# Hybrid decoder block on one core: high parts first in the products of sums, and the opening stage written in another order

## The chip, the cores and the metric

The kernel runs on one core of one Trainium2 chip. The metric is the time of one launch in device microseconds. Before the change it was 1389.92 us, the median of three runs (1389.33 to 1391.17).

## The reference

One decoder layer for 1024 positions of width 1024, in float32. Cut to what matters here:

```python
h = rms_norm(x, mix_norm_g)
z_a, q, k, v, gate_logits = jnp.split(h @ w_in, splits, axis=-1)
y_a = chunked_spatial_gating(gelu(z_a), gmlp_norm_g, w_spatial, b_spatial)
q, k = apply_partial_rope(q, cos, sin), apply_partial_rope(k, cos, sin)
y_b = dilated_mixture_attention(q, k, v)
merged = sigmoid(g_a) * (y_a @ w_branch_a) + sigmoid(g_b) * (y_b @ w_branch_b)
x = x + merged @ w_out
a, val = jnp.split(rms_norm(x, ffn_norm_g) @ w_up, 2, axis=-1)
x = x + (gelu(causal_dwconv3(a)) * val) @ w_down
return rms_norm(x, final_norm_g)
```

## The kernel before

**Numbers in two parts.** A float32 operand is split into a high part (a copy in the matmul's type, written by ScalarE) and a low part (operand minus high, written by VectorE, in later stages by GpSimd too). A product of a 512-deep slice is 12 matmuls into one PSUM bank: for each of 4 slices of 128 rows the passes high·high, high weight·low input, low weight·high input. The helper `to_parts` (from line 164) writes both parts of a weight.

**Fewer products.** The large projections use seven products of half-size blocks instead of eight. They are called P1, P6, P2, P7, P5, P4, P3. Their left operands are blocks of the input (A11, A12, A22) or sums of blocks (S1 to S4), their right operands blocks or differences of the weight. P2 accumulates into the bank of P1, P4 into that of P7 and P3 into that of P5. Between two such products VectorE or ScalarE has to fold the first one's result out of the bank: after P7 with `add(c22, c12, src)` (line 537), after P5 with `add(c22, c22, src)` (line 539), after P1 with a copy (line 530). So P4 waits for the fold of P7, and P3 for that of P5.

**The input projection** has pairs of 128 output columns. Pairs 0 and 1 are computed plainly, as four half products of 24 matmuls each (`plain_step`, line 562 on), because they need nothing but the raw input times the norm's gain; the row norms are applied later. From pair 2 on (`FIRST = 2`) `in_product` (line 498) computes the seven products. Its inputs are sums of the normalised input, so the norms have to be known: `square_row` and `root` (ScalarE and GpSimd), `diagonal` (four small diagonal matrices), `spread` (TensorE multiplies them by ones, so that each row's factor lies along the free side, tile `rs_bc`), `scale_x` (VectorE), `x_sum` and `x_sum_dma` (sums of blocks, two of them by a DMA that accumulates), `parts_of` (high and low parts of each block).

**What else stands in the opening.** `rot_tables` (line 2176) makes the sine and cosine tables of the rotary embedding: a chain of small VectorE steps, given out by `some(n)`; two sines on ScalarE; 16 small copies on ScalarE that widen the tables (`wide`, line 2238); and four turns, each four transposes on TensorE and a copy on ScalarE (`turns`, line 2255). `turn_v` (line 618) transposes the results of pairs 0, 1 and 2 by blocks into two shared PSUM tiles (`tr`), which ScalarE empties, with GELU for pairs 0 and 1 (line 628), by a copy for pair 2 (line 633). Then `norm_v` (squares on ScalarE, two GpSimd steps, a scaling on VectorE) and `spatial` (small matmuls into the same two PSUM tiles, emptied by VectorE, line 669).

**What sets the order.** Each engine runs its instructions in one order. On TensorE the order is that of the program throughout (`pe_order`). On VectorE and ScalarE it is the written one while `ordered` is open, that is through `beginning()` and the first seven products of pair 2 (`ORDERED = 6`). After that a scheduler orders these two engines, until a written order is opened again later (the opening of the up projection has one). `after(lag, fn)` queues work that is written `lag` ticks later; `tick()` comes every six matmuls of a product. `meanwhile(i)` is called after product i of the seven-product order. SyncE issues the loads in the order written. The up projection (`up_product`, line 1776) has the same seven products, its opening (`beginning_up`, from line 1889) in a written order: `up_ahead(loads, ops)` runs loads and weight parts ahead, `low(n)` writes n low parts that are waiting.

Of the kernel before, what the change touches and what calls it, by code (L numbers as in the profile page):

```python
# [20 lines left out]
P = 128  # L21
# [72 lines left out]
def block_kernel(  # L94
# [61 lines left out]
        return ap.bitcast(F32)  # L156

    PASSES = ((0, 0), (0, 1), (1, 0))


    waiting = []
# [45 lines left out]
    def after(lag, fn):  # L207
        pending.setdefault(clock[0] + lag, []).append(fn)
# [53 lines left out]
    def in_load(n, which):  # L262
        st = wt.tile([P, KT, P], F32, name=f"wr_{n}_{which}", tag="wr")
        nc.sync.dma_start(st, w_in[2 * n + which])
        raws[n, which] = st
# [63 lines left out]
    def load_x(h, kts):  # L329
        for kt in kts:  # L330
            nc.sync.dma_start(x_half(kt, h), xt[kt, :, h * HALF : (h + 1) * HALF])
# [4 lines left out]
    def load_rows(h):  # L336
        for b in range(4):
            nc.sync.dma_start(rows_of[b], x_t[:, 4 * h + b, :])
# [6 lines left out]
        load_x(0, range(k * QK, (k + 1) * QK))  # L345
    in_load(0, 1)
    load_x(1, range(KT))
    in_load(1, 0)
    load_rows(0)
    in_load(1, 1)  # L350

    nc.vector.memset(mhalf, -0.5)
# [41 lines left out]
    def quarter(i, j, kt):  # L394
        return X[:, j * QK + kt, (lower, upper)[i]]
# [36 lines left out]
    def parts_of(name, kts=range(QK)):  # L432
        i, j = {"A11": (0, 0), "A12": (0, 1), "A22": (1, 1), "S1": (1, 1), "S2": (0, 0),
                "S3": (1, 0), "S4": (0, 1)}[name]
        srcs = [Z[:, kt] if name == "S1" else quarter(i, j, kt) for kt in range(QK)]
        staggered((lambda: None, *in_left(name, kt, srcs[kt])) for kt in kts)
# [17 lines left out]
    def scale_x(h, kt, bc):  # L454
        xs = x_half(kt, h)
        nc.vector.scalar_tensor_tensor(xs, xs, chan[:, kt : kt + 1], bc, ALU.mult, ALU.mult)
# [41 lines left out]
    def in_product(n, name):  # L498
        opened = name not in SHARED
        if not opened:  # L500
            acc = in_banks[n, SHARED[name]]
        elif name == "P1" or n >= 3:
            acc = acc_tile(f"in_{n}_{name}")
        else:
            acc = ps_d.tile([P, HALF], F32, name=f"in_{n}_{name}", tag="dn")
        in_banks[n, name] = acc
        op = in_ops.pop((n, name))
        for kt in range(QK):
            for i, (w, a) in enumerate(PASSES):
                nc.tensor.matmul(  # L510
                    acc, op[:, w, kt, :], left[LEFT[name], kt][:, a, :],
                    start=opened and kt == 0 and i == 0,
                    stop=kt == QK - 1 and i == 2,
                    skip_group_check=not opened,
                )
            if kt % 2 == 1:
                tick()
        kind, _ = PAIRS[n]
        func = FUNC.get(kind, AF.Copy)
        src = in_turn(n, acc)  # L520
        c11, c12, c21, c22 = (c_half(n, i, h) for h in range(2) for i in range(2))
        add = nc.vector.tensor_tensor

        def final(i, h, t):
            if func != AF.Copy:
                nc.scalar.activation(t, t, func)
            in_final(n, i, h)

        if name == "P1":
            nc.scalar.activation(c12, src, AF.Copy)  # L530
        elif name == "P6":
            add(c12, c12, src, ALU.add)
        elif name == "P2":
            nc.scalar.activation(c11, src, func)
            in_final(n, 0, 0)
        elif name == "P7":
            add(c22, c12, src, ALU.add)  # L537
        elif name == "P5":
            add(c22, c22, src, ALU.add)
            final(1, 1, c22)  # L540
        elif name == "P4":
            add(c21, c12, src, ALU.add)
            final(0, 1, c21)
        else:
            add(c12, c12, src, ALU.add)
            final(1, 0, c12)
# [31 lines left out]
    def plain_final(n, h, i):  # L578
        nc.scalar.activation(c_half(n, i, h), plain_banks[n, h, i], AF.Copy)
# [468 lines left out]
    def beginning():  # L1048

        chain, wide, turns = rot_tables(  # L1050
            nc, lent, [[YC[:, i, lower], YC[:, i, upper]] for i in range(2)],
            tr_tile, ident, positions, YC,
        )
        chain = iter(chain)

        def some(n):
            for _, fn in zip(range(n), chain):
                fn()

        def weight(n, k, i):  # L1060
            hi, lo = plain_op(n, k, i)
            hi()
            lo()

        raw = {(h, kt): raw_left(h, kt) for h in range(2) for kt in range(KT)}

        def raw_parts(h, kt):
            for fn in raw[h, kt]:
                fn()

        def product(n, h, i, ks=(0, 1)):
            for k in ks:
                for kt in range(QK):
                    plain_step(n, h, i, k, kt)

        warm_up(12)
        some(5)
        for k in range(2):
            weight(0, k, 0)
            for kt in range(k * QK, (k + 1) * QK):  # L1080
                raw_parts(0, kt)
            product(0, 0, 0, (k,))
        some(2)
        weight(0, 0, 1)
        weight(0, 1, 1)
        plain_final(0, 0, 0)
        product(0, 0, 1)
        for kt in range(KT):
            raw_parts(1, kt)
        product(0, 1, 0)  # L1090
        plain_final(0, 0, 1)
        weight(1, 0, 0)
        weight(1, 1, 0)
        for b in range(4):
            square_row(0, b)
        load_rows(1)
        root(0)
        some(14)
        diagonal(0)
        plain_final(0, 1, 0)  # L1100
        weight(1, 0, 1)
        weight(1, 1, 1)
        product(0, 1, 1, (0,))
        for kt in range(QK):
            plain_step(0, 1, 1, 1, kt)
            if kt == 2:
                bc0 = spread(0)
        for kt in range(KT):
            scale_x(0, kt, bc0)
        plain_final(0, 1, 1)  # L1110
        for b in range(4):
            square_row(1, b)
        root(1)
        parts_of("A11")
        product(1, 0, 0)
        diagonal(1)
        bc1 = spread(1)
        for kt in range(QK):
            scale_x(1, kt, bc1)
            scale_x(1, kt + QK, bc1)  # L1120
            x_sum(1, kt)
            if kt % 2 == 1:
                x_sum_dma(3, kt // 2)
        plain_final(1, 0, 0)
        product(1, 0, 1)
        plain_final(1, 0, 1)
        parts_of("A12")
        in_ahead(0, 9, 2)
        product(1, 1, 0)
        plain_final(1, 1, 0)  # L1130
        for kt in range(2):
            x_sum(2, kt)
        parts_of("S2", range(2))
        product(1, 1, 1)
        in_ahead(0, 9, 3)
        for kt in range(2, QK):
            x_sum(2, kt)
        parts_of("S2", range(2, QK))
        plain_final(1, 1, 1)
        for k in range(2):  # L1140
            x_sum_dma(4, k)
        return some, wide, turns

    def meanwhile(i):
        if i == 0:
            parts_of("S3")
        elif i == 1:
            parts_of("S1")
        elif i == 2:
            parts_of("A22")  # L1150
        elif i == 3:
            parts_of("S4")
            x_stack.close()
            zv["pool"] = zv_stack.enter_context(
                tc.tile_pool(name="zvp", bufs=1, reuse_waits="tile")
            )
            open_zv()
            for b in range(0, NB, 2):
                after(1 + b // 2, lambda b=b: turn_v(1, C[1], b))
                after(5 + b // 2, lambda b=b: turn_v(0, C[0], b))  # L1160
        elif i == ORDERED:
            some(99)
            for fn in wide:
                fn()
        elif i == ORDERED + 2:
            for fn in turns:
                fn()

    ordered = ExitStack()
    ordered.enter_context(  # L1170
# [3 lines left out]
    for i, (n, name) in enumerate(in_order):  # L1174
        in_ahead(i, 9, 4 if i else 2)
        if PAIRS[n][0] == "zu" and name == "P1":
            for c in range(2 * PAIRS[n][1], 2 * PAIRS[n][1] + 2):
                nc.sync.dma_start(ya[:, c, :], mixd[c])
        in_product(n, name)
        meanwhile(i)  # L1180
        if i == ORDERED:
            ordered.close()
# [593 lines left out]
    def up_product(ff, name, beside=None):  # L1776
# [6 lines left out]
            acc = banks[ff, SHARED[name]]  # L1783
        banks[ff, name] = acc
        op = ops.pop((ff, name))
        for kt in range(QK):
            for i, (w, a) in enumerate(PASSES):
                nc.tensor.matmul(  # L1788
                    acc, op[:, w, kt, :], left[LEFT[name], kt][:, a, :],
                    start=opened and kt == 0 and i == 0,  # L1790
                    stop=kt == QK - 1 and i == 2,
                    skip_group_check=not opened,
                )
            if kt % 2 == 1:
                tick()
        u2, v, c21, c12 = u2s[ff % 2], vs_[ff % 2], c21s[ff % 2], c12s[ff % 2]
        ge0, ge1 = ge_of(ff, 0), ge_of(ff, 1)
# [91 lines left out]
    def beginning_up():  # L1889
# [79 lines left out]
        up_product(2, "P7")  # L1969
        up_ahead(18, 16)  # L1970
        up_product(2, "P5")
        up_ahead(18, 17)
        low(1)
        first_taps(2)
        up_product(2, "P4", lambda: up_ahead(20, 19))
        low(1)
# [334 lines left out]
```

## Time and profile before

| | |
|---|---|
| three runs | 1389.33, 1391.17, 1389.92 us |
| the profiled execution | 1391.06 us |
| its span, first to last instruction | 1389.1 us |
| mean granted TensorE clock | 0.996 |
| instructions | 19247 |
| HBM | 167.77 MB read, 64.29 MB written |

Views give times in us from the span's start. A row of the timeline gives start, duration, engine, line, operation, output and inputs, shape and count; in brackets the time that the engine had been idle and what ended that. Durations of one instruction overlap the next one's by a little, since the ends of pipelined instructions are modelled: twelve matmuls that start 0.227 us apart are shown as 2.88 us. A row of the windows gives for each engine the busy time and the number of instructions in that stretch, then the granted clock and the DMA engines' share. PEq, SPq and the like are sequencers; PEld is TensorE loading weights.

### The profile page before, as it was taken

How to read it: one execution, taken by the hardware profiler on the slowest of the kernel's cores; microseconds unless marked ns; L12 is line 12 of the kernel's file. 1: busy time of each engine (PE TensorE's matmuls, PEld its weight loads, DVE VectorE, ACT ScalarE, POOL GpSimd, SP SyncE). 2: the span in 40 equal slices, each digit the busy share in tenths (PEclk: the TensorE clock that was granted, in tenths of full speed). 3: DMA queues.
4: the chain of work that ended last, by engine and by line, in shares of the span. 5: the costliest groups of instructions: out<-in, count | busy, mean ns of one | idle time of the engine just before them, and what ended most of it. 6: DMA issues, size and time to landing. Idle time of an engine off the chain costs nothing.

```text
span 1389.1 us, 19247 instructions
## 1 busy us (share of the span) xinstructions
PE 1364.6 (98%) x6434; PEld 1130.7 (81%) x6434; DVE 1030.6 (74%) x1880; ACT 655.1 (47%) x1289; POOL 298.1 (21%) x295
## 2 busy tenths in 40 slices
PE   9889999999999999999999999999999999999997
PEld 7767888888888888888788878888888888888886
DVE  7868677686877987867889887766766667676674
ACT  7583355555544333634646444333433335455443
POOL 0111000000221000120001146655566553000003
PEclk9999999999999999999999999999999999999999
DMA  9424535354435997694843133333323327986563
GB/s 352 89 65 130 167 109 169 115 167 134 130 116 193 329 307 256 216 300 140 287 133 104 39 117 103 106 107 113 107 103 110 122 84 254 385 322 221 196 206 122
DMA packets 143875, 237.01 MB, mean 171 GB/s; under 512 B 13728, under 2 KB 57504, under 8 KB 143776
## 3 DMA queue, kind: packets, MB, share of 16 engines
q1 hardware_dynamic: 141248, 231.53, 49.5%
q0 software_dynamic: 1088, 2.10, 0.9%
q10 hardware_dynamic: 1440, 2.16, 0.4%
q8 instruction: 51, 0.84, 0.2%
q14 instruction: 48, 0.39, 0.1%
HBM read 167.77 MB, written 64.29 MB: 167 GB/s over the span
## 4 chain that ended last, share of the span: by engine, by line
PE 85%; DVE 6%; ACT 3%; issue 2%; POOL 2%; DMA 2%; SPq 0%; POOLq 0%; ACTq 0%; DVEq 0%
PE in_P L510 25%; PE uP L1788 19%; PE dn L2046 13%; PE up L1788 8%; PE pa L1260 5%; PE wo_P L1621 4%; PE pl L571 2%; PE pu L1767 2%; PE pb L1260 1%; PE pu L851 1%; DMA ld<-scr 1%; PE pp L835 1%; DVE G L166 1%; PE pm L660 1%; POOL st L903 1%
## 5 line engine op out<-in xcount | busy, mean ns | idle before, releaser
L510 PE MATMUL in_P<-R,G 128*128 128x512 f32 x1008 | 243.8, 394 | 1.8 <-ACT C L530 1.8
L510 PEld LDWEIGHTS in_P<-R,G 128*128 128x128 f32 x1008 | 185.4, 188 | 38.5 <-ACT C L530 2.2
L2046 PE MATMUL dn<-R 128*128 128x512 f32 x924 | 209.6, 389 | 0.0
L2046 PEld LDWEIGHTS dn<-R 128*128 128x128 f32 x924 | 173.4, 188 | 36.0
L165 ACT ACTIVATE G<-wr 128x512 fp32r<-128x512 f32 x126 | 79.1, 630 | 150.4 <-PE in_P L510 114.4
L165 ACT ACTIVATE R<-up 128x512 fp32r<-128x512 f32 x130 | 78.8, 627 | 125.1 <-DVE up L278 40.9
L510 PE MATMUL in_P<-G,G 128*128 128x512 f32 x504 | 124.1, 397 | 2.3 <-DVE C L537 2.3
L1788 PE MATMUL up<-G,R 128*128 128x512 f32 x504 | 121.4, 391 | 1.7 <-DVE R L166 1.7
L1788 PE MATMUL uP<-G,R 128*128 128x512 f32 x504 | 121.2, 389 | 0.0
L1788 PE MATMUL uP<-R 128*128 128x512 f32 x504 | 121.1, 389 | 0.0
L1788 PEld LDWEIGHTS up<-G,R 128*128 128x128 f32 x504 | 94.5, 188 | 22.7 <-DVE R L166 2.2
L510 PEld LDWEIGHTS in_P<-G,G 128*128 128x128 f32 x504 | 93.7, 190 | 21.1 <-ACT G L405 2.5
L1788 PEld LDWEIGHTS uP<-G,R 128*128 128x128 f32 x504 | 94.5, 188 | 19.8 <-issue 0.2
L1788 PEld LDWEIGHTS uP<-R 128*128 128x128 f32 x504 | 94.6, 188 | 19.6
L166 DVE TENSOR_TENSOR G<-wr,G 128x512 fp32r<-128x512 f32 x126 | 87.9, 699 | 24.2 <-ACT G L165 24.0
L166 POOL TENSOR_TENSOR R<-up,R 128x512 fp32r<-128x512 f32 x55 | 84.0, 1527 | 74.5 <-ACT R L165 74.5
L166 DVE TENSOR_TENSOR R<-up,R 128x512 fp32r<-128x512 f32 x75 | 63.0, 841 | 16.1 <-ACT R L165 15.9
L165 ACT ACTIVATE R<-db 128x512 fp32r<-128x512 f32 x77 | 48.1, 626 | 56.3 <-PE dn L2046 45.3
L166 DVE TENSOR_TENSOR R<-db,R 128x512 fp32r<-128x512 f32 x77 | 53.7, 701 | 25.8 <-ACT R L165 25.7
L1260 PE MATMUL pa<-R,G 128*128 128x512 f32 x288 | 67.9, 389 | 0.0
L1260 PEld LDWEIGHTS pa<-R,G 128*128 128x128 f32 x288 | 54.1, 188 | 11.2
L510 PE MATMUL in_P<-G 128*128 128x512 f32 x252 | 62.2, 393 | 0.0
(279 smaller groups left out, 2396.5 us busy)
## 6 DMA issues: line engine op xcount, KB each, us to landing
wr<-in_w_in_dram SPq DMA_DIRECT2D x45, 512.0 KB, 4.1
up<-in_w_up_dram SPq DMA_DIRECT2D x44, 512.0 KB, 3.5
dA<-gd SPq DMA_DIRECT2D x55, 256.0 KB, 5.1
wd<-in_w_down_dram SPq DMA_DIRECT2D x44, 256.0 KB, 5.5
wT<-wd SPq DMA_DIRECT2D x44, 256.0 KB, 3.7
dS<-gS SPq DMA_DIRECT2D x44, 256.0 KB, 4.2
db<-wT SPq DMA_DIRECT2D x44, 256.0 KB, 4.2
gd<-Y SPq DMA_DIRECT2D x42, 256.0 KB, 2.0
```

The lines of the kernel that those rows point to most:

```text
L165: nc.scalar.activation(hi, src, AF.Copy)
L166: fn = lambda: lo_eng.tensor_tensor(lo, src, f32(hi), ALU.subtract)
L510: nc.tensor.matmul(acc, op[:, w, kt, :], left[LEFT[name], kt][:, a, :], start=opened and kt == 0 and i == 0, stop=kt == QK - 1 and i == 2, ...
L571: nc.tensor.matmul(acc, plain_ops[n, k, i][:, w, kt, :], raw_x[h, k * QK + kt][:, a, :], start=k == 0 and kt == 0 and p == 0, stop=k == 1 ...
L660: nc.tensor.matmul(pm[:, o : o + P], v[:, c * P : (c + 1) * P], wspT[:, c * 2 // 3, :], start=True, stop=True,)
L835: nc.tensor.transpose(pp[:, i * P : (i + 1) * P], self.pr[:, h, s * P : (s + 1) * P], ident)
L851: nc.tensor.matmul(pu[:, h * HD : (h + 1) * HD], self.pT[:, i, :], vt[:, h * HD : (h + 1) * HD], start=i % n == 0, stop=i % n == n - 1,)
L1260: nc.tensor.matmul(acc, unit[a][kt // 4][:, kt % 4, :], two(R, 8 * h + kt)[:, b, :], start=n == 0 and i == 0, stop=n == len(kts) - 1 and i ...
L1621: nc.tensor.matmul(acc, left[LEFT[name], kt][:, a, blk * P : (blk + 1) * P], out_ops[s][:, w, :], start=name not in SHARED and kt == 0 and ...
L1767: nc.tensor.matmul(acc, plain_up[which, k][:, w, kt, :], left[f"A{h + 1}{k + 1}", kt][:, a, :], start=n == 0 and i == 0, stop=n == KT - 1 ...
L1788: nc.tensor.matmul(acc, op[:, w, kt, :], left[LEFT[name], kt][:, a, :], start=opened and kt == 0 and i == 0, stop=kt == QK - 1 and i == 2, ...
L2046: nc.tensor.matmul(accs[blk], dops[s][:, 0, a, blk * P : (blk + 1) * P], dops[s][:, 1, w, :], start=SEQ[j] not in CONTINUES and kt == 0 an ...
```

## The change

Within each product of `in_product` and `up_product` the twelve matmuls come in another order: four high·high, then four low weight·high input, then four high weight·low input. In the opening, two loads change places and several steps move: the weights of pair 1, the first spread, the squares of the second half, the parts of A11, the second diagonal, the second spread, and P1 of pair 2, which now stands between the two halves of the last plain product. The transposes of pairs 1 and 0 are written four ticks later, the parts of S1 and A22 and the four table turns at other products. In the up projection one weight is loaded and split earlier.

```diff
+    HIGH_FIRST = [(w, a, kt) for w, a in ((0, 0), (1, 0), (0, 1)) for kt in range(D // P // 2)]
...
     load_x(1, range(KT))
+    load_rows(0)
     in_load(1, 0)
-    load_rows(0)
     in_load(1, 1)
...
-        for kt in range(QK):
-            for i, (w, a) in enumerate(PASSES):
-                nc.tensor.matmul(
-                    acc, op[:, w, kt, :], left[LEFT[name], kt][:, a, :],
...
-            if kt % 2 == 1:
+        for i, (w, a, kt) in enumerate(HIGH_FIRST):
+            nc.tensor.matmul(
+                acc, op[:, w, kt, :], left[LEFT[name], kt][:, a, :],
...
+            if i % 6 == 5:
                 tick()
...
         plain_final(0, 0, 1)
-        weight(1, 0, 0)
-        weight(1, 1, 0)
         for b in range(4):
             square_row(0, b)
         load_rows(1)
         root(0)
-        some(14)
+        some(5)
+        weight(1, 0, 0)
+        weight(1, 1, 0)
+        some(11)
         diagonal(0)
         plain_final(0, 1, 0)
...
             plain_step(0, 1, 1, 1, kt)
-            if kt == 2:
+            if kt == 0:
                 bc0 = spread(0)
         for kt in range(KT):
             scale_x(0, kt, bc0)
+        for b in range(2):
+            square_row(1, b)
         plain_final(0, 1, 1)
-        for b in range(4):
+        for b in range(2, 4):
             square_row(1, b)
         root(1)
-        parts_of("A11")
+        a11 = [in_left("A11", kt, quarter(0, 0, kt)) for kt in range(QK)]
+        for hi, lo in a11[:2]:
+            hi()
+            lo()
+        diagonal(1)
+        for hi, lo in a11[2:]:
+            hi()
+            lo()
         product(1, 0, 0)
-        diagonal(1)
+        plain_step(1, 0, 1, 0, 0)
         bc1 = spread(1)
...
-        product(1, 0, 1)
+        for n in range(1, KT):
+            plain_step(1, 0, 1, n // QK, n % QK)
...
-        product(1, 1, 1)
+        product(1, 1, 1, (0,))
         in_ahead(0, 9, 3)
+        in_product(FIRST, "P1")
+        product(1, 1, 1, (1,))
...
     def meanwhile(i):
         if i == 0:
             parts_of("S3")
-        elif i == 1:
+            in_ahead(1, 9, 4)
             parts_of("S1")
-        elif i == 2:
+        elif i == 3:
             parts_of("A22")
-        elif i == 3:
             parts_of("S4")
...
-                after(1 + b // 2, lambda b=b: turn_v(1, C[1], b))
-                after(5 + b // 2, lambda b=b: turn_v(0, C[0], b))
+                after(5 + b // 2, lambda b=b: turn_v(1, C[1], b))
+                after(9 + b // 2, lambda b=b: turn_v(0, C[0], b))
         elif i == ORDERED:
             some(99)
             for fn in wide:
                 fn()
-        elif i == ORDERED + 2:
-            for fn in turns:
-                fn()
+        elif ORDERED + 2 < i < ORDERED + 7:
+            turns.pop(0)()
...
-        in_product(n, name)
+        if i:
+            in_product(n, name)
...
         up_product(2, "P5")
-        up_ahead(18, 17)
-        low(1)
+        up_ahead(20, 18)
+        low(2)
         first_taps(2)
```

The loop of `up_product` changes as that of `in_product` does.

More of the change, by code (lines that the diff above doesn't have):

```diff
@@ L507, in in_product @@
         op = in_ops.pop((n, name))
-        for kt in range(QK):
-            for i, (w, a) in enumerate(PASSES):
-                nc.tensor.matmul(
-                    acc, op[:, w, kt, :], left[LEFT[name], kt][:, a, :],
[L512 to L515, printed above, removed]
-            if kt % 2 == 1:
+        for i, (w, a, kt) in enumerate(HIGH_FIRST):
+            nc.tensor.matmul(
+                acc, op[:, w, kt, :], left[LEFT[name], kt][:, a, :],
+                start=opened and i == 0,
+                stop=i == len(HIGH_FIRST) - 1,
+                skip_group_check=not opened,
+            )
+            if i % 6 == 5:
                 tick()
@@ L1785, in up_product @@
         op = ops.pop((ff, name))
[L1786 to L1794, printed above, removed]
+        for i, (w, a, kt) in enumerate(HIGH_FIRST):
+            nc.tensor.matmul(
+                acc, op[:, w, kt, :], left[LEFT[name], kt][:, a, :],
+                start=opened and i == 0,
+                stop=i == len(HIGH_FIRST) - 1,
+                skip_group_check=not opened,
+            )
+            if i % 6 == 5:
                 tick()
```

## The prediction, made before the changed kernel ran

> **What bounds the kernel.** I read the page first, then the waits of TensorE, then windows of the first 140 us, then the timeline of each engine there, and from the built program of the changed kernel the order of each engine and what each instruction waits for. Page, waits and windows:
>
> ```profile
> PE 1364.6 (98%) x6434; PEld 1130.7 (81%) x6434; DVE 1030.6 (74%) x1880; ACT 655.1 (47%) x1289; POOL 298.1 (21%) x295
> PE 85%; DVE 6%; ACT 3%; issue 2%; POOL 2%; DMA 2%; SPq 0%; POOLq 0%; ACTq 0%; DVEq 0%
> PE in_P L510 <- DVE C L537: 2.3, 1, 2.3
> PE in_P L510 <- ACT C L530: 1.8, 1, 1.8
> PE rs_bc L391 <- ACT C L385: 1.8, 1, 1.8
> PE up L1788 <- DVE R L166: 1.7, 1, 1.7
> PE rot L2255 <- ACT YC L2256: 1.4, 1, 1.4
> PE vt L623 <- ACT V L628: 1.3, 1, 1.3
> PE rot L2255 <- ACT YC L2238: 1.1, 1, 1.1
> 76.00:83.00 7.00, 5.72 (x19) 4.26 (x18) 5.96 (x10) 3.49 (x9) 0.00 (x0) 0.52 0.26 87
> 90.00:100.00 10.00, 7.31 (x45) 5.67 (x44) 4.58 (x16) 9.66 (x30) 0.00 (x0) 1.00 0.00 1
> 120.00:130.00 10.00, 10.00 (x60) 7.75 (x59) 9.47 (x22) 1.75 (x3) 0.00 (x0) 1.00 0.44 124
> ```
>
> TensorE is busy for 98% of the span, and from about 100 us on it hardly stops. So whatever the opening gains or loses reaches the end unchanged, unless a later wait swallows it. Six of the waits lie between 38 and 99 us and make 1.8 + 1.8 + 2.3 + 1.3 + 1.1 + 1.4 = 9.7 us. The clock was 0.52 for the 7 us behind two of them: busy 5.72 us at half speed, about 2.5 us lost. I put 1 us more for the modelled ends, since each wait is counted from an end that lies 0.16 us (2.88 - 12 x 0.227) behind the time when the next matmul could have started. That is about 13 us which the change can win there, and 1.7 us at the up projection.
>
> **The change part by part. Order inside a product.** It touches 2 x 1764 = 3528 matmuls.
>
> ```profile
> L510 PE MATMUL in_P<-R,G 128*128 128x512 f32 x1008 | 243.8, 394 | 1.8 <-ACT C L530 1.8
> L2046 PE MATMUL dn<-R 128*128 128x512 f32 x924 | 209.6, 389 | 0.0
> L1621 PE MATMUL wo_P<-R,G 128*128 128x512 f32 x72 | 19.9, 400 | 0.4 <-ACT Y L1589 0.4
> 19.33 2.88 PE L571 MATMUL pl<-G 128*128 128x512 f32 x12
> 22.05 2.88 PE L571 MATMUL pl<-R,G 128*128 128x512 f32 x12
> ```
>
> Two of three neighbours in the old order share their weight, in the new one none does. The down projection (line 2046) has neighbours that never share it, at 389 ns: so I take 0. The ends are 5 ns less for the input products (1764 x 5 ns = 9 us gained) and the 400 ns of line 1621 (3528 x 6 ns = 21 us lost). What the order does is to need the low weight at the fifth matmul instead of the third and the low inputs at the ninth to twelfth. The high inputs are all needed by the fourth (0.7 us in) instead of the tenth. A product takes 22.05 - 19.33 = 2.72 us.
>
> **Rows ahead of pair 1's weights.**
>
> ```profile
> 24.64 1.06 ACT L366 ACTIVATE YC<-YC 128x1024 f32<-128x1024 f32 x1 [1.39 <-DMA YC<-in_x_dram]
> 18.00:28.00 10.00, 10.00 (x46) 8.29 (x45) 7.20 (x20) 8.48 (x17) 0.92 (x2) 1.00 1.03 396
> 27.28 1.03 POOL L374 TENSOR_TENSOR rs_x<-me_x,mhalf 128x4 f32<-128x4 f32 x1
> 20.68 1.29 DVE L559 TENSOR_TENSOR G<-wr,G 128x512 fp32r<-128x512 f32 x2
> 23.79 0.62 DVE L2193 TENSOR_TENSOR ones<-ones 128x128 f32<-128x128 f32 x2
> 28.35 0.88 DVE L383 TENSOR_SCALAR C<-ident,rs_x 128x128 f32<-128x128 f32 x4 [2.63 <-POOL rs_x L374]
> 27.49 2.20 PE L571 MATMUL pl<-R,G 128*128 128x512 f32 x9
> 29.53 1.05 PE L391 MATMUL rs_bc<-C,ones 128*128 128x128 f32 x8
> ```
>
> The queue is full there (396 GB/s, 1.3 us per 512 KB tile). In the trace the third row tile lands at 24.6, with pair 1's weight ahead of it. In the changed kernel the fourth lands at 24.6, the last square ends at 25.8 instead of 26.8, and the weight lands at 25.7. But VectorE now has the weight's low parts ahead of 11 table steps, and those ahead of the first diagonal. It waits for the weight's high part (25.8 + 0.6), does two low parts (1.29) and 11 steps (some 0.28 each, 3.1 with the gaps): 30.8 instead of 28.35. TensorE reaches the spread after three matmuls of the half that starts at 27.49, at 28.2, and waits until about 31.0. **+2.8 us**, where the trace has no wait. Cover for this there is none: all of the changed TensorE order stands behind.
>
> **Second spread, and P1 between the halves.** The squares of the second half are no longer queued behind the eviction alone, and the second spread comes three matmuls later. By my count its diagonals end at 39.5 and TensorE arrives at 40.2, so the 1.8 us there go. P1 ends 2.7 us before the plain product does, time enough for its eviction (0.6 us, line 530), so the next 1.8 us go too. The last plain half ends at 59.5.
>
> **VectorE's chain to the folds.** The stretch from the second scaling to the fold of P5 has the same instructions as before, in nearly the same order:
>
> ```profile
> 39.90 1.41 DVE L456 SCALAR_TENSOR_TENSOR X<-X,chan,rs_bc 128x512 f32<-128x512 f32 x2 [0.78 <-PE rs_bc L391]
> 57.73 1.29 DVE L465 TENSOR_TENSOR X<-X,YC 128x512 f32<-128x512 f32 x2
> 66.23 2.50 DVE L412 TENSOR_TENSOR G<-YC,G 128x512 fp32r<-128x512 f32 x4 [1.32 <-ACT G L411]
> 77.92 0.68 DVE L539 TENSOR_TENSOR C<-C,in_P 128x512 f32<-128x512 f32 x1
> 75.14 1.96 PE L510 MATMUL in_P<-G,G 128*128 128x512 f32 x6 [2.33 <-DVE C L537]
> ```
>
> It begins at 41.4 instead of 39.90 (the spread ends at 41.2), and is 1.5 us late until 59.25. Then a table load on ScalarE no longer stands ahead of S1's high parts, and the 1.3 us wait goes. From there every 128x512 step is 0.6 us (four in 2.50): P7's fold ends at 72.2, four low parts of A22, four of S4 and one weight follow, and P5's fold ends at 78.2. TensorE, no longer held before, ends P7 at 67.7 and P5 at 70.4. P4 waits for P7's fold: **+1.9**. It ends at 75.0, and P3 waits for P5's fold: **+3.3**. In the trace this fold was as late (77.92), but transposes and the second half of P4 filled the time.
>
> **Transposes.** They now start in P3, and the table steps come among their evictions:
>
> ```profile
> 91.67 0.83 ACT L628 ACTIVATE V<-vt,rs_x 128x256 f32<-128x256 f32 x2
> 93.01 1.28 ACT L2232 ACT_TABLE_LOAD   x1
> 94.30 0.26 ACT L2232 ACTIVATE ones<-ones 128x64 f32<-128x64 f32 x1
> 95.09 3.28 ACT L2238 ACTIVATE YC<-ones 128x128 f32<-128x128 f32 x16
> ```
>
> After P5's fold come three weight differences (2.2 us), a high part, a low part, P4's fold, a GELU and another high part, each step 0.5 to 0.6; the first block's two GELU evictions end at 84.2. TensorE has turned two blocks by 82.0 and needs the first PSUM tile back: **+2.3**. It then reaches the seventh block at 90.6. The tile for it holds the fourth block of pair 1, and in the built order ScalarE empties that in two halves with the table work between: sine table load from 87.9 (1.3), sines when VectorE's 17 remaining steps end at 90.2, GELU table load (1.3, a load more than before), first half, all 16 widening copies (3.3), second half. That ends at 91.7 + 0.4 + 3.3 + 0.4 = 95.8. **+5.2 us.** Even with the sines free at once it would be 4.4.
>
> ```profile
> 100.70 0.84 ACT L192 ACTIVATE junk_v<-V 128x768 bf16<-128x768 f32 x1
> 102.00 0.57 POOL L196 TENSOR_TENSOR rs_v<-me_v,mhalf 128x1 f32<-128x1 f32 x1
> 110.41 1.64 DVE L669 SCALAR_TENSOR_TENSOR V<-pm,chan,b_bc 128x128 f32<-128x128 f32 x6
> ```
>
> ScalarE then has the squares (1.0 us each with their read) ahead of the last evictions: the first table turn waits until 103.5, **+1.2**. The eighth square ends at 111.6, the seventh at 110.6; GpSimd adds 1.1, and VectorE, in order, empties the first spatial tile only at 113.5 to 115. The third table turn needs that tile: **+1.9**, and the fourth **+0.4**. Later spatial blocks come 4.8 us apart and VectorE has half a microsecond to spare in each, so no more waits. Sum of the new waits: 2.8 + 1.9 + 3.3 + 2.3 + 5.2 + 1.2 + 1.9 + 0.4 = 19.0; less 13.0: **+6.0 us**.
>
> **Clock.** In the trace waits of 1.8 us cost no clock, and 2.3 followed by 1.3 did: 6.8 us at half. So the 5.2 us wait should halve it for some 3.5 us; of the 1.7 lost the next wait swallows 1.2: **+0.5**. The first wait (2.8) may halve it for as long; that delays VectorE's chain by 1.6. It depends on where the wait falls, so I carry **+1.0**, with ends 0 and 1.6. Losses between 70 and 90 us vanish in the 5.2.
>
> The Trainium skill, TensorE: Matmul & The Clock Gate, "HAM oscillation", asks for idle gaps over about 3.4 us before the clock falls. The trace fell after a gap of 2.3. By the page the +1.0 would be 0.
>
> The Trainium skill, ScalarE: Activation LUTs, "What ACT_TABLE_LOAD costs", adds a drain of about 1.4 us to each load. Here the sine follows its load 1.29 us after that began, so no drain shows; by the page the two loads would add about 2.8.
>
> **Up projection.** The weight of P1 of block 4 gets its low part ahead of the taps.
>
> ```profile
> 816.71 2.57 PE L1788 MATMUL up<-G,R 128*128 128x512 f32 x10 [1.74 <-DVE R L166]
> 818.80 0.78 ACT L1721 ACTIVATE Y<-up,chan 128x512 f32<-128x512 f32 x1 [1.50 <-DVE edge L1755]
> 824.60 2.93 PE L1788 MATMUL up<-G,R 128*128 128x512 f32 x12
> ```
>
> The 1.7 us go; the taps behind start 2 us later, and P2 of block 4 (at 824.60 in the trace) becomes the next late one, by about 0.5. **-1.2**, with ends -1.9 and 0.
>
> **Sum.** 6.0 + 0.5 + 1.0 - 1.2 = +6.3 us. On the profiled execution (1391.06 us: span 1389.1 and 2.0 around it) that is 1397.4. The median of the runs lies 1.1 lower, at 1389.92, and the comparison goes by medians: **1396.2 us**.
>
> **Rivals.** *The weight lands early.* If the loads don't land in the order of issue and pair 1's weight is there by about 23 us, the diagonal isn't held: the first wait and its clock go, VectorE's chain starts 2.5 us earlier, and everything to 96 us is as much earlier. That is 6.3 - 2.5 - 1.0 = +2.8, near 1392.7, within 0.2%: not slower. Against it: 396 GB/s with row tiles that land one by one. 12%. *The matmuls get quicker.* If sharing a weight costs the input products their 5 ns, high-first wins 9 us: 1387.2, faster or at the edge. It decides whether line 510 goes from 394 to 389. Against it: the up products share it too, at 389 to 391 mostly. 6%. *The clock falls more often.* If it is also low at 31 us in full and two windows long behind the 5.2 us wait, 1.7 + 1.6 more: about 1399. 14%. *The page's drain:* 1399 as well, 2%. *Shared weights help:* 1417, 2%. *The waits don't sum*, because a step isn't where I have it: within 1 us of before, 4%. My forecast, 1393 to 1399: 60%.
>
> **Range and chances.** 1390.5 to 1400. About 0.2%, 2.8 us, is what a measurement tells from no change. Faster 7%, the same 14%, slower 79%.
>
> **What would show it.** A wait of some 2.8 us ahead of the first spread near 28 us, put down to line 386 of the new file; waits on the folds of P7 and P5 near 71 and 75; the longest one, some 5 us, ahead of a transpose at 90 us, ended by an eviction of ScalarE with the 16 copies just before it; a table load more; no wait before P2 of pair 2; TensorE unbroken from 125 us on and the same spacing of matmuls. If the transposes aren't held at 90 us, the forecast is wrong by most of its size.

## The result: 10 us slower, and the profile after

| | median | all runs | against before of the same call |
|---|---|---|---|
| before | 1391.17 us | 1389.33 to 1394.89, 5 runs | |
| changed | 1401.83 us | 1399.04 to 1405.86, 5 runs | 1.0072 [1.0045, 1.0100] |
| changed, again beside other kernels (changed_again) | 1401.39 us | 1398.08 to 1402.37, 6 runs | 1.0070 [1.0056, 1.0084] |

The direction was forecast, the size was not: +9.7 to +10.7 us instead of +6.3, above the top of the range (1400). (The forecast of 1396.2 stands on a median of before of 1389.92; with two more runs that median is 1391.17, and the 1.25 us between them are part of the 5.6 by which the result lies above the forecast.) The profiled execution of the changed kernel took 1405.86 us (span 1404.1), the slowest of its runs, at a mean clock of 0.989; the other four had 0.992 to 0.995. Two lines of its page (busy times, and the granted clock in 40 slices of 35 us) and its waits of TensorE:

```profile
PE 1374.7 (98%) x6434; PEld 1138.5 (81%) x6434; DVE 1032.1 (74%) x1880; ACT 654.6 (47%) x1290; POOL 299.6 (21%) x295
PEclk9978999999999999999999999999999999999999
```

```profile
PE vt L625 <- ACT V L630: 6.4, 2, 4.3
PE in_P L512 <- DVE C L541: 3.2, 2, 3.0
PE rot L2268 <- DVE V L671: 2.7, 2, 2.1
PE rs_bc L394 <- DVE C L386: 2.4, 1, 2.4
PE in_P L512 <- ACT G L414: 1.8, 1, 1.8
PE up L1801 <- ACT t L1814: 1.5, 1, 1.5
PE uP L1801 <- DVE R L169: 1.0, 1, 1.0
```

The waits of before on the second spread and on P1's copy are gone, and the new ones stand where the prediction put them. One has another cause: P4's wait of 1.8 us is put down to line 414, ScalarE's high parts of A22, where the prediction had P7's fold (line 539). The two end within 0.1 us of each other:

```profile
71.30 2.17 ACT L414 ACTIVATE G<-X 128x512 fp32r<-128x512 f32 x4
72.72 0.68 DVE L539 TENSOR_TENSOR C<-C,in_P 128x512 f32<-128x512 f32 x1
```

Busy time of TensorE rose by 10.1 us with the same 6434 matmuls. That is clock, not work: by the windows below, some 20 us more ran at half clock, which makes 10 us of busy time. The timeline of TensorE shows the waits one by one (start, duration, in brackets the idle time before and what ended it):

```profile
30.62 1.93 PE L394 MATMUL rs_bc<-C,ones 128*128 128x128 f32 x8 [2.43 <-DVE C L386]
...
73.55 3.00 PE L512 MATMUL in_P<-G,G 128*128 128x512 f32 x12 [1.80 <-ACT G L414]
79.56 2.90 PE L512 MATMUL in_P<-G 128*128 128x512 f32 x6 [3.01 <-DVE C L541]
...
88.27 0.65 PE L625 MATMUL vt<-ident,C 128*128 128x128 f32 x4 [2.11 <-ACT V L630]
...
100.76 1.97 PE L625 MATMUL vt<-ident,C 128*128 128x128 f32 x8 [4.33 <-ACT V L630]
...
120.31 1.08 PE L2268 MATMUL rot<-ident,YC 128*128 128x128 f32 x4 [2.13 <-DVE V L671]
121.05 5.47 PE L512 MATMUL in_P<-G,G 128*128 128x512 f32 x12
```

Look at the durations behind the waits: six matmuls take 2.90 us behind 79.56, and twelve take 5.47 us behind 121.05, where twelve at full clock take 2.88. The windows give the clock there (busy time and instructions of PE, PEld, DVE, ACT and POOL; then granted clock, DMA share, GB/s). Four stretches of the changed kernel, then two of before:

```profile
26.00:34.20 8.20, 5.77 (x23) 4.69 (x22) 7.53 (x22) 4.33 (x9) 0.00 (x0) 0.79 1.02 408
78.60:92.30 13.70, 10.63 (x36) 8.51 (x37) 9.77 (x20) 5.50 (x11) 1.57 (x4) 0.63 0.17 48
92.30:105.90 13.60, 9.27 (x44) 7.67 (x42) 3.05 (x12) 13.34 (x36) 1.35 (x3) 0.75 0.01 2
119.50:140.00 20.50, 19.13 (x96) 14.96 (x97) 13.15 (x33) 3.57 (x6) 0.00 (x0) 0.83 0.40 110
```

```profile
70.00:78.60 8.60, 4.99 (x24) 3.44 (x23) 8.51 (x15) 6.37 (x15) 0.00 (x0) 0.86 0.36 122
78.60:92.30 13.70, 13.70 (x70) 11.59 (x70) 9.95 (x22) 10.49 (x24) 1.66 (x4) 0.84 0.17 49
```

Finer windows show only 1.00 and 0.50 or 0.51. So a mean clock of 0.63 over 13.7 us is 2 x 0.37 x 13.7 = 10.1 us at half speed, 0.79 over 8.2 us is 3.4, 0.75 over 13.6 us is 6.8, 0.83 over 20.5 us is 7.0: about 27 us at half clock in the opening. The two rows of before (0.86 over 8.6 us, 0.84 over 13.7) make 2.4 + 4.4 = 6.8 us.

The 27 us belong to the slowest run. The profile of changed_again, the same kernel at 1401.43 us, has 17: the clock was 0.51 from 77.9 to 81.4, from 95.0 to 101.9 and from 115.5 to 122.4 us, behind P3's wait, the longest wait and the wait at the third table turn. Its first wait (2.05 us) and its wait at the third block (2.11 us) cost no clock.

### The profile page after: what moved, and what is told of

Its sections match the earlier page's. It is cut to its first block, busy times and chain, and to the rows that moved or that the text cites. A ratio compares the mean times of both kernels' runs of the same rounds, so it can differ in the third digit from the quotient of the medians.

```text
span 1404.1 us, 19217 instructions
## 1 busy us (share of the span) xinstructions
PE 1374.7 (98%) x6434; PEld 1138.5 (81%) x6434; DVE 1032.1 (74%) x1880; ACT 654.6 (47%) x1290; POOL 299.6 (21%) x295
```

## The experiments

Theory A: the waits of the opening and the half clock behind them make the time. Rivals: only the waits count (W), the order inside a product costs (B) or gains (C), the losses before 100 us are swallowed by the longest wait (D) or by the one ahead of P4 (E). Each kernel ran beside the kernel before.

### The order inside a product

The kernel before with `for i, (w, a, kt) in enumerate(HIGH_FIRST)` in `in_product` and `up_product`, nothing else.

> The kernel before, with the new order inside a product and nothing else. Theory A (the opening's waits and the half clock behind them make the 10.7 us; the order is worth nothing): within 1.5 us of before, near 1391, and the medians of the product lines unchanged. Rival B (the order itself costs, because no two neighbours share a weight): most of the 10.7 us is already here, 1396 or more. Rival C (it gains 5 ns a matmul on the input products): 1382 to 1386.

Measured 1391.11 us (before 1391.60), ratio 0.9997 [0.9986, 1.0008]. The groups of its two product lines:

```profile
L510 PE MATMUL in_P<-R,G 128*128 128x512 f32 x1008 | 244.5, 395 | 0.7 <-ACT C L530 0.7
L1787 PE MATMUL uP<-R 128*128 128x512 f32 x504 | 121.1, 389 | 0.0
```

394 ns became 395, and 389 stayed. The order is worth nothing, as forecast; B and C fall. (The 397 ns of the changed kernel's line 512 are the half clock: in fill_right below, which has hardly any, the same group takes 394.)

### Undoing one part of the change

```diff
  # lags_back: transposes and turns as before
-                after(5 + b // 2, lambda b=b: turn_v(1, C[1], b))
-                after(9 + b // 2, lambda b=b: turn_v(0, C[0], b))
+                after(1 + b // 2, lambda b=b: turn_v(1, C[1], b))
+                after(5 + b // 2, lambda b=b: turn_v(0, C[0], b))
...
-        elif ORDERED + 2 < i < ORDERED + 7:
-            turns.pop(0)()
+        elif i == ORDERED + 2:
+            for fn in turns:
+                fn()
  # first_back: loads, pair 1's weights, table steps, first spread as before
-    load_rows(0)
     in_load(1, 0)
+    load_rows(0)
...
+        weight(1, 0, 0)
+        weight(1, 1, 0)
         for b in range(4):
             square_row(0, b)
         load_rows(1)
         root(0)
-        some(5)
-        weight(1, 0, 0)
-        weight(1, 1, 0)
-        some(11)
+        some(14)
...
-            if kt == 0:
+            if kt == 2:
                 bc0 = spread(0)
```

> The changed kernel with the transposes of pairs 1 and 0 four ticks earlier again and the four table turns together again, as before. Theory A: the waits of 2.1 and 4.3 us ahead of transposes and of 2.1 and 0.6 ahead of the table turns go, the waits of before (1.3 + 1.1 + 1.4) partly return, net about -5; and the half clock after 88 us goes (about 7 us lost there), so 8 to 12 us less than the changed kernel, 1390 to 1394. If the waits count and the clock does not (theory W): about 5 us less, near 1397.

> The changed kernel with the order of loads, pair 1's weights, the table steps and the first spread as before. Theory A: the first wait (2.4 us) and the half clock from 30.8 to 34.2 (1.7 us) go; VectorE's chain to the folds starts about 2.5 us earlier, TensorE 4, so the fold waits grow by about 1.5 and what stays is 2.5 us less, near 1399; up to 4 less if a clock window behind the folds goes too. Rival D (all that comes before the transposes is swallowed by the wait of 4.3 us): no change, 1400 to 1403.

lags_back: 1395.97 us, 5.4 less than the changed kernel (1401.39 in changed_again; the medians of before in the two calls are 1391.60 and 1391.66). first_back: 1396.76 us, 4.6 less, so D falls: the first wait is paid in full, and more than its 2.4 us. How much of the rest is half clock was not taken apart. But lags_back did not lose its waits as expected, so that its time, nearer to the 1397 of W than to the 1390 to 1394 of A, decides nothing between them. With the parts of S1 and A22 still at their new places the transposes stand at others (lags_back, TensorE):

```profile
77.36 1.12 PE L625 MATMUL vt<-ident,C 128*128 128x128 f32 x4 [4.05 <-ACT V L630]
...
98.10 1.11 PE L625 MATMUL vt<-ident,C 128*128 128x128 f32 x4 [5.46 <-ACT V L630]
```

So where the parts stand and where the transposes stand must be judged together; undoing one alone says little of it.

### Adding one part after the other

```diff
  # middle_alone: before, and this
             scale_x(0, kt, bc0)
+        for b in range(2):
+            square_row(1, b)
         plain_final(0, 1, 1)
...
-        product(1, 1, 1)
+        product(1, 1, 1, (0,))
         in_ahead(0, 9, 3)
+        in_product(FIRST, "P1")
+        product(1, 1, 1, (1,))
```

middle_alone is before with the new order inside a product, the second spread and A11 as in the change, and P1 between the halves. middle_and_up adds the up projection's part, turns_and_parts_back the loads, weights and first spread; lags_back above adds the parts of S1 and A22, the changed kernel the transposes and turns.

> As middle_and_up, but with the up projection's loads and low parts as before as well. By the trace of the changed kernel the up projection's part costs about 0 to 0.8 us (waits of 1.5 and 1.0 for one of 1.7): 0.4 less than middle_and_up. By the prediction's term it gains 1.2: 1.2 more than middle_and_up. Against the kernel before: within 1.5 us (the gains at the second spread and P2 given back at the folds), or up to 3.6 less if they are not.

> The changed kernel with the loads, pair 1's weights, table steps, first spread, parts of S1 and A22, transposes and table turns as before. New are the order inside a product, the second spread and P1 between the plain halves, and the up projection. Theory A: no new wait in the opening, the waits of 1.8 us (second spread) and 1.8 us (P2) gone but given back at the folds, since VectorE's chain ends these: 1390 to 1393. If it stays above 1396, another part of the change costs.

> The changed kernel with the transposes, the table turns and the parts of S1 and A22 as before: beside middle_and_up (1390.6) only the loads, pair 1's weights, the table steps and the first spread are new. Theory A: the first wait (2.4 us) comes back, delays VectorE's chain to P7's fold by as much, so nothing swallows it; with the half clock behind it in some runs 2.4 to 4.5 more than middle_and_up, 1393 to 1395. Rival E (the 4.1 us wait ahead of P4 swallows it): 1390 to 1391.5. What then lies between this and lags_back (1396.0) is the parts' place; what lies between lags_back and the changed kernel (1401.4) is the transposes' and turns'.

> The changed kernel itself, as it is, beside the other three on the same chip, for a firmer median (five runs so far, 1399.0 to 1405.9). All theories: 1400 to 1403.

| kernel | median | less its own before | ratio [interval] |
|---|---|---|---|
| order_alone | 1391.11 | -0.5 | 0.9997 [0.9986, 1.0008] |
| middle_alone | 1388.99 | -2.7 | 0.9983 [0.9975, 0.9992] |
| middle_and_up | 1390.64 | -1.0 | 0.9997 [0.9988, 1.0005] |
| turns_and_parts_back | 1393.18 | +2.3 | 1.0015 [1.0005, 1.0024] |
| lags_back | 1395.97 | +4.4 | 1.0028 [1.0015, 1.0041] |
| changed_again | 1401.39 | +9.7 | 1.0070 [1.0056, 1.0084] |

The steps: order -0.5 (nothing that can be told), middle -2.2, up projection +1.65, first wait +3.3, parts +2.1, transposes and turns +5.4. Each carries 1.5 to 2 us of doubt, so that the +1.65 and the +2.1 are hardly clear of it.

The middle part gains, though TensorE stands 4.1 us for P7's fold behind it: it does not give everything back, since the fold itself comes earlier than in before, where P4 started at 75.14. TensorE and VectorE of middle_alone:

```profile
72.83 2.90 PE L510 MATMUL in_P<-G,G 128*128 128x512 f32 x6 [4.09 <-DVE C L537]
```

```profile
72.00 0.68 DVE L537 TENSOR_TENSOR C<-C,in_P 128x512 f32<-128x512 f32 x1
```

With the first wait added (turns_and_parts_back) the wait ahead of P4 is as long, but 4.6 us later, and so is the fold. The wait there cannot swallow the one before it, because the fold's chain on VectorE hangs on the same spread; E falls:

```profile
30.71 1.16 PE L394 MATMUL rs_bc<-C,ones 128*128 128x128 f32 x8 [2.46 <-DVE C L386]
...
77.44 2.90 PE L512 MATMUL in_P<-G,G 128*128 128x512 f32 x6 [4.09 <-DVE C L539]
```

```profile
76.62 0.68 DVE L539 TENSOR_TENSOR C<-C,in_P 128x512 f32<-128x512 f32 x1
```

Part of the loss comes back later in the kernel all the same: set against the same instruction in middle_and_up, TensorE stands 4.5 us later up to 377 us and 2.6 us or less from 587 us on. What gives it back was not taken apart.

The up projection's part is told by TensorE of middle_alone (first fence) and of middle_and_up (second):

```profile
815.23 2.12 PE L1800 MATMUL up<-G,R 128*128 128x512 f32 x8 [1.33 <-DVE R L167]
...
822.68 2.93 PE L1800 MATMUL up<-G,R 128*128 128x512 f32 x12
```

```profile
822.78 2.99 PE L1802 MATMUL up<-G,R 128*128 128x512 f32 x12 [1.72 <-ACT t L1815]
...
838.50 2.11 PE L1802 MATMUL uP<-R 128*128 128x512 f32 x8 [0.94 <-DVE R L169]
```

The wait for the weight goes, TensorE reaches P2 of block 4 that much earlier, and then stands there for ScalarE's copy of P1 (line 1815), which had been early enough before and now comes 1.3 us later, behind the convolution's taps (822.15 against 820.82): P2 starts at nearly the same time in both. On top comes a new wait of 0.94 us for a low part 16 us later, and the product behind that starts at 840.44 against 839.05.

### Filling the waits

These kernels keep every wait and its cause, but let TensorE multiply the identity into an unused PSUM tile meanwhile, so that little but the clock should differ (the unused tile takes a turn among the buffers of its pool). Part of fill_right:

```diff
+        if (p, b) in ((2, 4), (0, 0)):
+            fill = acc_tile(f"fill_{p}")
+            for _ in range(8 if p else 16):
+                nc.tensor.matmul(fill[:, :P], ident, ident, start=True, stop=True)
         pt = tr_tile(f"vt_{p}_{b}")
```

and alike ahead of the first spread, P4, P3 and the third table turn.

> The changed kernel with extra matmuls of the identity into unused PSUM tiles ahead of the six long waits of the opening (9, 6, 11, 9, 17, 9 of some 0.24 us each), so that TensorE is busy while it would stand; the results are unused and nothing waits for them but TensorE itself. It leaves every wait's cause alone. Theory A: the half clock behind the waits goes (27 us at half down to 7 or less), some 11 us of lost time, of which other waits swallow about a third to a half: 5 to 8 us less than the changed kernel, 1394 to 1397. Theory W (only the waits count): no change, or up to 2 us more.

> As the run named fill, but with the extra matmuls ahead of the transposes where the trace of the changed kernel shows the waits: the third and the eighth block in TensorE's order (8 and 16 matmuls); 9, 6, 11 and 8 ahead of the first spread, P4, P3 and the third table turn. In the run named fill, 26 of the 61 stood where there was no wait (5.8 us added) and two waits were left bare. Theory A (half clock behind the waits costs several us): 4 to 7 us less than the changed kernel, 1395 to 1398, with a mean clock of 0.996 or more in all runs. Theory W (only the waits count, since a later wait swallows what the half clock loses): within 1.5 us of the changed kernel, 1400 to 1403.

fill missed its aim: 1402.55 us. Two fillings, at (1, 4) and (0, 4), stood where there was no wait and added their own time. With these at the right blocks, fill_right took 1395.32 us (1393.48 to 1396.23), 6.1 less than the changed kernel of the same call, at a mean clock of 0.998 to 0.999 in its runs. W falls. Its timeline of TensorE, where the bracket now holds only what the filling left over, and then ScalarE at the table work, in fill_right and in the changed kernel:

```profile
71.66 2.98 PE L518 MATMUL in_P<-G,G 128*128 128x512 f32 x12 [0.47 <-ACT G L416]
77.67 1.63 PE L518 MATMUL in_P<-G 128*128 128x512 f32 x6 [0.59 <-DVE C L547]
...
83.68 0.66 PE L635 MATMUL vt<-ident,C 128*128 128x128 f32 x4 [0.32 <-ACT V L640]
...
94.90 1.14 PE L635 MATMUL vt<-ident,C 128*128 128x128 f32 x8 [1.05 <-ACT V L640]
```

```profile
81.23 0.63 ACT L168 ACTIVATE G<-wt 128x512 fp32r<-128x512 f32 x1 [0.90 <-PE in_P L518]
...
87.55 1.28 ACT L2259 ACT_TABLE_LOAD   x1
...
94.39 0.45 ACT L640 ACTIVATE V<-vt,rs_x 128x256 f32<-128x256 f32 x1
```

```profile
85.82 0.63 ACT L168 ACTIVATE G<-wt 128x512 fp32r<-128x512 f32 x1 [3.61 <-PE in_P L512]
...
93.69 1.28 ACT L2245 ACT_TABLE_LOAD   x1
...
97.07 3.28 ACT L2251 ACTIVATE YC<-ones 128x128 f32<-128x128 f32 x16
100.25 0.46 ACT L630 ACTIVATE V<-vt,rs_x 128x256 f32<-128x256 f32 x1
```

ScalarE waits for TensorE ahead of the table work: the weight split at 85.82 needs the end of P3's matmuls. P3 itself starts 1.9 us later in the changed kernel (79.56 against 77.67), runs at half clock, and so this step comes 4.6 us later, the table load 6.1, and the eviction that ends the longest wait 5.9.

That is the slowest run again. In changed_again P3 starts only 0.3 us later than in fill_right (77.94), but with the half clock from there on the same three steps of ScalarE are each 1.85 us later:

```profile
83.08 0.63 ACT L168 ACTIVATE G<-wt 128x512 fp32r<-128x512 f32 x1 [2.48 <-PE in_P L512]
...
89.40 1.28 ACT L2245 ACT_TABLE_LOAD   x1
...
96.24 0.45 ACT L630 ACTIVATE V<-vt,rs_x 128x256 f32<-128x256 f32 x1
```

The same for before, first ahead of P4 alone, then ahead of all six waits of its opening:

> The kernel before with 9 extra matmuls ahead of P4, where its trace shows 2.3 us of wait and 6.8 us of half clock behind. Theory A: 1.5 to 2.5 us less than before, 1389 to 1390, with less spread between runs. Theory W: no change. Together with fill_right (1395.3) it gives the change's cost with hardly any half clock in either: about 6, which is what the prediction summed for the waits alone.

> The kernel before with extra matmuls ahead of all six waits of its opening (6 ahead of the second spread, 6 ahead of P2, 9 ahead of P4, 5 ahead of the third transposed block, 3 and 4 ahead of the first and third table turn). In before_filled the half clock had only moved to 95.9 us, behind the two waits at the table turns. Theory A: with these filled too the mean clock is 0.998 or more and the time 1387.5 to 1389.5, 2 to 4 us less than before; then fill_right (1395.3) lies 6 to 8 us above it, which is the price of the change without any half clock. Theory W: no gain, 1390 to 1392.

before_filled: 1390.51 us, ratio 0.9989 [0.9977, 1.0000]: hardly a gain, because the half clock came behind the table turns instead (0.51 from 95.9 to 102.8 us). before_all_filled: 1388.75 us, 0.9984 [0.9974, 0.9994], at a clock of 0.998 in its profile. So the half clock costs before 2.3 us and the changed kernel 6.1, and without it the change costs 1395.32 - 1388.75 = 6.6 (5.9 if each is set against before of its own call). Each of these carries about 2 us of doubt.

Last, middle_alone with its two long waits filled (15 matmuls ahead of P4, 7 ahead of the second turn):

> middle_alone (1389.0) with extra matmuls into an unused PSUM tile ahead of P4 (15) and of the second table turn (7), where its trace shows waits of 4.1 and 2.2 us, each with a half clock behind it (6.8 and 3.4 us long). Theory A: the half clock goes and 2 to 4 us with it, 1385 to 1387. Theory W: no gain, 1388.5 or more.

1385.15 us (1384.10 to 1386.80), 0.9953 [0.9940, 0.9967] of before: the best of all here, better than both kernels. The windows behind its two waits, in middle_alone and then in middle_filled, clock 0.57 and 0.72 against 1.00:

```profile
70.00:78.00 8.00, 4.83 (x13) 3.56 (x14) 7.93 (x14) 5.04 (x11) 0.00 (x0) 0.57 0.39 129
...
93.00:99.00 6.00, 4.02 (x17) 3.51 (x18) 0.69 (x1) 5.48 (x17) 0.36 (x2) 0.72 0.19 53
```

```profile
70.00:78.00 8.00, 5.64 (x36) 4.56 (x36) 7.93 (x14) 5.05 (x11) 0.00 (x0) 1.00 0.39 130
...
93.00:99.00 6.00, 5.01 (x32) 4.05 (x31) 1.31 (x2) 5.97 (x16) 1.11 (x4) 1.00 0.28 89
```

## Why the prediction was too low

| part of the sum | predicted | measured, and how |
|---|---|---|
| waits of the opening, without clock | 19.0 - 10.5 = +8.5 | 6.6 less the up projection's 1.65 = +4.9 |
| half clock in the opening | 0.5 + 1.0 - 2.5 = -1.0 | 6.1 - 2.3 = +3.8 |
| up projection | -1.2 | +1.65 (middle_and_up less middle_alone) |
| sum | +6.3 | +10.4 |

(10.5 is the 13 that the prediction removes, less its 2.5 of clock. The 10.4 stands beside +9.7 and +10.7 measured directly; the calls' own medians of before differ by 0.6.)

**The steps that failed.** First: "Losses between 70 and 90 us vanish in the 5.2". They did not, because the end of that wait is not fixed: ScalarE, which ends it, waits for TensorE's P3 itself, as its rows above show. Half clock at 79 us moves both ends of the 5.2, the later one by 1.85 us in changed_again. Second, the clock's term: it was put behind two waits, at +1.5 us in all. The profiled run shows it in all four stretches above, also behind the waits of 3.0, 2.1 and 2.1 us, and changed_again in three, of which the prediction had one, that behind the longest wait. Taken out by filling, it is worth 6.1 us. The prediction went by the length of a wait (1.8 us cost none, 2.3 did); the last section shows what the traces say instead. The rival "the clock falls more often" had this in kind, but at 1399 it was still bound to those two places. Third, the up projection: "P2 of block 4 (at 824.60 in the trace) becomes the next late one, by about 0.5" names the right product, but the wait is 1.7 us, no less than what had been won, and a further one of 0.9 was not seen.

**What held.** The order inside a product costs nothing. The first spread started at 30.6 us after a wait of 2.4 (predicted 31.0 and 2.8). P4, P3, the third block and the longest wait: predicted at 72.3, 78.3, 84.3 and 95.8; in fill_right, without half clock, at 71.7, 77.7, 83.7 and 94.9. (The block that the prediction calls the seventh is the eighth in TensorE's order, counting those of pair 2; its tile is the one of pair 1's fourth block, as said.) The waits on the second spread and P2 went, the table load more came, the 16 copies stand inside the longest wait. Two sizes were too large: the first table turn's 1.2 did not come, and the longest wait was 4.3 instead of 5.2. The new waits of the profiled run add up to 16.4 us where the prediction had 19.0. That the opening's waits net only 4.9 and not 8.5 was luck for the sum: it hid 3.6 of the 7.7 us by which the clock (4.8) and the up projection (2.9) were missed. And "whatever the opening gains or loses reaches the end unchanged" held only nearly: changed_again stands 10.6 us behind before at 124 us, 9.4 at 811 us and 10.6 again at the end, the last 1.2 from the up projection.

The Trainium skill, TensorE: Matmul & The Clock Gate, "HAM oscillation", which wants gaps over about 3.4 us before the clock falls, does not agree with these traces: it was at half behind gaps of 2.1 and 2.4 us. By the page the changed kernel would have lost clock behind its 4.3 us alone.

What stays open: which of the moved parts of S1 and A22 makes the 2.1 us of their step, and what gives back 1 to 2 us between about 380 and 700 us. Neither was taken apart.

## What to carry to other kernels

A wait in a chain that feeds later waits is mostly paid; before writing that a later wait swallows a loss, follow the instruction that ends it back, and see whether it hangs on the engine that was delayed. Where a matmul engine must stand for 2 us or more, price the time behind the wait at half clock too, and try filling the wait with idle matmuls: here it gave 2 to 6 us for a few lines where every long wait of the opening was filled, and next to nothing (before_filled, 0.4 us) where one alone was, because the half clock moved behind the next. Removing one wait only shows the next one: find the second latest input before counting the gain.

## What the hardware showed

The half clock comes in whole stretches of about 3.4 or 6.8 us (0.50 from 39.3 to 42.6 us in order_alone), and a gap of 1.75 us ahead of the second spread was enough there, while the wait of 1.8 us at the same place cost no clock in the profiled run of before. Two rows of order_alone's timeline of TensorE and one of its windows:

```profile
38.04 1.38 PE L392 MATMUL rs_bc<-C,ones 128*128 128x128 f32 x8 [1.75 <-ACT C L386]
39.17 4.12 PE L571 MATMUL pl<-R,G 128*128 128x512 f32 x10
```

```profile
39.30:42.60 3.30, 3.30 (x9) 2.56 (x9) 3.10 (x5) 0.05 (x1) 0.00 (x0) 0.50 0.00 0
```

The two lie at the edge of a rule that the granted clock of the traces shows. In all 14 traces it changes only at points that lie whole multiples of 3.41 us from each other: at 30.8, 34.2, 78.6, 85.4, 88.8, 92.3, 99.1, 105.9, 119.6 and 126.4 us in the profiled run of the changed kernel, at 78.0, 81.4, 95.0, 101.8, 115.5 and 122.3 in changed_again. What counts is how much idle time falls between two neighbours of this grid. There are 5603 such stretches at full clock in the 14 traces. In 23 of them TensorE stood idle, as the profile shows it, for 1.80 us or more, and each of the 23 was followed by half clock. Of the other 5580 only three were, with 1.35, 1.38 and 1.75 us; the longest idle time that cost nothing is 1.79. The clock was full again behind stretches with 0.48 us idle or less, and stayed at half behind 0.63 or more.

So the first wait of the changed kernel (2.43 us) lay whole between 27.4 and 30.8 us in the profiled run and cost clock; in changed_again a grid point at 30.2 cut its 2.05 us into 1.64 and 0.41, and it cost none. The grid lies elsewhere in each execution, so a wait of about 2 us costs clock in one and not in the next. No run here moved a wait against the grid, so this is read from the traces and not tested.

It is also a part of the spread between runs: the five runs of the changed kernel go from 1399.04 us at a mean clock of 0.995 to 1405.86 at 0.989. Those of fill_right lie within 2.8 us, the changed kernel's within 4.3 and 6.8.
